# A two-layer diffusion backbone: SSD chunk exponentials issued one chunk step earlier, modulation row sums queued behind VectorE's last evacuation

## The chip, the core and the metric

One program on one core of a Trainium2 chip. A core has a matrix engine (TensorE, PE in the profile; its weight loads are PEld), VectorE (DVE), ScalarE (ACT), GpSimd (POOL) and a queue of transfers (SyncE, SP), which run beside each other and wait for one another through semaphores. Each takes its own instructions in the order in which the program queued them. The metric is the device time of one execution in microseconds (us); a kernel's time is the median of its runs.

## What is computed

The reference runs two post-norm layers over 512 latent tokens and 256 context tokens of width 1024. Layer 0 mixes tokens with gated linear attention, layer 1 with a bidirectional Mamba-2 scan (SSD); each is followed by a squared-ReLU MLP of width 4096. Every sub-layer's input is scaled and shifted, and its output gated, by vectors that come from one linear map of the conditioning. Cut to what matters here:

```python
m_l = split((silu(c) @ ada_w[i] + ada_b[i]), 6)      # latent stream
m_c = split((silu(c_ctx) @ ada_w[i] + ada_b[i]), 6)  # context stream
h = layer_norm(alpha * h + m[2] * mixer(h * (1 + m[1]) + m[0]))
h = layer_norm(alpha * h + m[5] * square(relu((h * (1 + m[4]) + m[3]) @ w1)) @ w2)
# SSD, per chunk and head; j sums over the chunk's tokens
decay = exp(where(mask, cum_i - cum_j, -inf))
y = (C_i . B_j) * decay * (x_j dt_j)  +  C_i . exp(cum_i) . state
```

There are six modulation vectors per layer (m[0] to m[5]), and two streams.

## The kernel before

All matrices are kept transposed, 128 features on the partitions and 768 tokens (512 latent, then 256 context) along the free axis. Each large product is made of three float32r products of a high and a low part: the weight is split into `wh` and `wl` (`split_to`, L211: the copy on ACT, the subtraction on VectorE), the activation into `xh` and `xl`, or `rh` and `rl` in the MLP. `prod` (L253) runs the three terms over the 8 tiles of the contraction. Weights are loaded through four `raw` buffers by SyncE, and `wh` and `wl` have three buffers each. Products land in four PSUM banks, two for a block of 768 columns.

**How work is interleaved.** The program is traced once, in Python. `worked(n)` (L188) is called after every matmul of the large products and counts their columns; each 768 columns are one unit. After a number of units that the running generator asked for, the next step of the `side` queue is traced (a LayerNorm, or the inner part of an SSD group). Every `pace[0]` units one step of the `background` queue is traced. A scheduler then gives each engine's instructions out in the order in which they become ready in its own model of the machine, earlier traced ones first among those that are ready. So an instruction that depends on little can be queued long before the place at which it was traced. `tc.issue_after(ins)` takes that freedom: what a block traces on the engine of `ins` is queued behind `ins`. It is an order of issue, not a wait for the end of `ins`.

**The MLP** (`ffn`, L382). W1 blocks go through `f1` (L387): `prod`, then `f1_out` (L392): relu from PSUM on ACT (L403), its square on POOL into `rq`, one buffer (L404), the rounded square `rh` on ACT (L405), the remainder `rl` on VectorE (L406). Batches of 8, 8, 8, 5 and 3 blocks of W1 (`bi` 0 to 4; the sizes of layer 0) are each followed by the matching part of W2 (`accum_proj`, L443), whose products are evacuated by `gated_add` (L438) with the gate of the modulation, on VectorE. In the first batch two blocks are held in PSUM, while the LayerNorm before finishes. The gate, vector (layer, 5), is asked for by `mod` (L205) at the end of the first batch; `mod` traces background steps until it is there.

**Row sums.** The modulation vectors after the first two are not made by TensorE. `ada_rows` (L143) is a background generator: for each of the eight 128-row parts of a vector it loads 128 rows of the transposed map (512 KB, three `rawa` buffers, one load ahead) and takes one multiply with row sum on VectorE per stream (L166), with the row of silu(c) broadcast in `srow`. During layer 0's mixer three vectors of layer 0 are made. At the start of layer 0's MLP the list [(0, 5), (1, 0) to (1, 5)] is queued: 56 steps, of two sums each for the first three vectors and of one for the last four, 80 sums in all. The pace is 21, then 15 after the two held blocks, then 22 from the end of the first batch on.

**The SSD layer** (`ssd_layer`, L771) has eight groups of four heads. `group(g)` (L920) projects and convolves B, C and two tiles of x (`conv`, L889: PSUM is copied out on ACT, L896, and the taps L905 and the gate L908 run on VectorE), then two gate tiles, and puts `inner(g)` (L938) on the side queue, so that it is traced between the projections of the next group. `evac[0]` always holds ACT's last evacuation. `inner` goes through four chunks of 128 latent tokens:

- `chunk_rows(c)` (L947) loads two rows of cumulated decay, broadcast over the partitions, into `L` tiles (ten buffers, two per chunk), and POOL masks them (L952). Chunks 0 and 1 are fetched at the start, chunk c + 2 in step c.
- `inter(i)` (L1020) multiplies with the running states and adds up `T`.
- `decays(c, L)` (L1032) takes the exponentials, 8 of 128x128 on ACT (L1039), with the other token's term as bias.
- `masks(c, L)` (L1041) adds the two directions on POOL (L1042) and multiplies by C.B on VectorE (L1043).
- `outputs(c, M)` (L1046) runs TensorE over the mask (L1050) and adds to `T` (L1053).

In the loop of L1058, step c traces the outputs of chunk c - 1, then the exponentials of chunk c behind `evac[0]`, then its masks. 14 units lie between steps (13 in the last group), and 4 before each `inter` (5).

Of the kernel before, what the change touches and what calls it, by code (L numbers as in the profile page):

```python
# [2 lines left out]

# [6 lines left out]
F32 = mybir.dt.float32  # L10
# [3 lines left out]
ALU = mybir.AluOpType  # L14
# [22 lines left out]
NLC = NL // P  # L37
# [23 lines left out]
def tile_backbone(ctx, tc, xT, cc, cr, vecs, rows, ada_w0, ada_wr, lnf, ffn_w1, ffn_w2,  # L61
                  gla_w_in, gla_w_v, gla_w_a, gla_a2, gla_w_out, ssd_w_in, ssd_w_dt, ssd_w_out, out):
    nc = tc.nc
# [28 lines left out]
    def part_of(ps, t0, n):  # L92
        return ps[t0 // NL][:, t0 % NL:t0 % NL + n]
# [17 lines left out]
    nc.gpsimd.memset(sT, 0.0)  # L111
    nc.scalar.activation(sT[:, :, 0:2], cin, AF.Silu)
    mods = {}

    def ada_block(src, dst, c0, rawf):
        j, b = dst.shape[1:3]
# [26 lines left out]
    def ada_rows(items, alloc, junk):  # L143
        srow = [alloc(s) for s in range(2)]
        for s in range(2):
            nc.sync.dma_start(srow[s], cr[s:s + 1, :].to_broadcast([P, D]))
            nc.scalar.activation(srow[s], srow[s], AF.Silu)
        def load(layer, m, b):
            raw = wpool.tile([P, D], F32, tag="rawa", name=nm("rawa"), bufs=3)
            nc.sync.dma_start(raw, ada_wr[48 * layer + 8 * m - 16 + b])  # L150
            return raw

        todo = [(layer, m, b) for layer, m in items for b in range(8)]
        raws = [load(*todo.pop(0))]
        yield
        for layer, m in items:
            streams = range(1 if layer and m > 1 else 2)
            t = ct([P, 8, 2], f"row{layer}{m}")
            nc.gpsimd.memset(t, 0.0)
            for b in range(8):  # L160
                if todo:
                    raws.append(load(*todo.pop(0)))
                raw = raws.pop(0)
                for s in streams:
                    o = raw if s == streams[-1] else junk()
                    nc.vector.scalar_tensor_tensor(o, raw, 1.0, srow[s], ALU.mult, ALU.mult, accum_out=t[:, b, s:s + 1])  # L166
                yield
            c0 = V_ADA + 48 * layer + 8 * m
            nc.vector.tensor_tensor(t, t, vec[:, c0:c0 + 8].unsqueeze(2).to_broadcast([P, 8, 2]), ALU.add)
            mods[layer, m] = t  # L170
# [28 lines left out]
    wait, pace = [0], [9]  # L199
# [182 lines left out]
    def ffn(layer, xs, acc, segs, pool, npre, presegs, restsegs, passes, after):  # L382
        W1, W2 = ffn_w1[layer], ffn_w2[layer]
        rs = {}
        NN = span(segs)[1]

        def f1(m, sg, hold=None):  # L387
            w, ps = hold or (weights(W1, m), mm_ps(sg))
            prod(ps, w, xs, sg, KT)
            f1_out(m, ps)  # L390

        def f1_out(m, ps):  # L392
            if m not in rs:
                rs[m] = (pool.tile([P, NN], F32R, tag="rs", name=nm("rh"), bufs=20),
                         pool.tile([P, NN], F32R, tag="rs", name=nm("rl"), bufs=20))
            rh, rl = rs[m]
            for piece in passes if m == DFF // P - 1 else (segs,):
                a, b = span(piece)
                eng = nc.gpsimd if piece is segs else nc.vector
                r = pool.tile([P, NN], F32, tag="rr", name=nm("rr"), bufs=2)  # L400
                q = pool.tile([P, NN], F32, tag="rq", name=nm("rq"), bufs=1)
                for (t0, n, _) in piece:
                    nc.scalar.activation(r[:, t0:t0 + n], part_of(ps, t0, n), AF.Relu)  # L403
                eng.tensor_mul(q[:, a:b], r[:, a:b], r[:, a:b])  # L404
                nc.scalar.activation(rh[:, a:b], r[:, a:b], AF.Square)  # L405
                nc.vector.tensor_sub(rl[:, a:b], q[:, a:b], rh[:, a:b].bitcast(F32))  # L406

        nlast = NN // 256
        h0 = 0
        for bi, nb in enumerate((8, 8, 8, 8 - nlast, nlast)):  # L410
            ms = range(h0, h0 + nb)
            if bi == 0:
                drain(1)
                held = []
                for m in ms[:npre]:
                    held.append((weights(W1, m), mm_ps(segs)))
                    prod(held[-1][1], held[-1][0], xs, presegs, KT)
                drain()
                for m in ms[:npre]:
                    f1(m, restsegs, held[m])  # L420
                pace[0] = 15
                ms = ms[npre:]
            if bi == 4:
                ws = pair_weights(W2, h0, nb,
                                  lambda j: [pool.tile([P, NN], F32R, tag="rs", name=nm("ws"), bufs=20) for _ in range(2)])
            for m in ms:
                f1(m, segs)
            ys = [rs[m] for m in range(h0, h0 + nb)]
            if bi == 0:
                gate = mod(layer, 5)  # L430
                pace[0] = 22
            if bi < 4:
                accum_proj(W2, h0, nb, ys, gate, acc, segs)
            else:
                accum_last(ws, ys, gate, acc, passes, after, early=None if layer == 0 else 5)
            h0 += nb

    def gated_add(acc, m, ps, gate, segs, src=None):  # L438
        for (t0, n, s) in segs:
            nc.vector.scalar_tensor_tensor(acc[m][:, t0:t0 + n], part_of(ps, t0, n), gate[:, m, s:s + 1],  # L440
                                           (src or acc)[m][:, t0:t0 + n], ALU.mult, ALU.add)

    def accum_proj(W, k0, kt, xs, gate, acc, segs, ms=range(KT)):  # L443
        for m in ms:
# [326 lines left out]
    def ssd_layer(xs, accd, acc0):  # L771
# [21 lines left out]
        with phase("st0") as tp:  # L793
# [14 lines left out]
            src = wload(ssd_w_dt)  # L808
            split_to(w[:, :, 0:64], w[:, :, 64:], src)
            ps = mm_ps()  # L810
# [24 lines left out]
            for c0, c1 in ((0, 4), (4, 6)):  # L835
# [3 lines left out]
                vc, n = v[:, c0:c1], c1 - c0  # L839
# [71 lines left out]
        evac = [None]  # L911
# [26 lines left out]
        def inner(g, fB, fC, fx, zs):  # L938
# [8 lines left out]
            def chunk_rows(c):  # L947
                L = [sp.tile([P, 4, P], F32, tag="L", name=nm("L"), bufs=LB) for _ in range(2)]
                for z in range(2):
                    nc.sync.dma_start(L[z].rearrange("p h i -> p (h i)"),  # L950
                                      crowc[z, c, g:g + 1].rearrange("g h i -> g (h i)").to_broadcast([P, 4 * P]))
# [7 lines left out]
            Rs, Ms = {c: chunk_rows(c) for c in range(2)}, {}  # L959
# [60 lines left out]
            def inter(i):  # L1020
                nc.scalar.activation(Es[i], Es[i], AF.Exp)
                for z in range(2):
                    E = Es[i][:, z]
                    ip = sm_ps([P, NL])
                    for c in range(NLC):
                        cs = slice(c * P, (c + 1) * P)
                        nc.tensor.matmul(ip[:, cs], ST[c][:, z, i * P:(i + 1) * P], fC[:, cs], start=True, stop=True)
                    nc.vector.tensor_mul(E if z else T[:, i], ip, E)
                nc.gpsimd.tensor_add(T[:, i], T[:, i], E)
                nc.vector.scalar_tensor_tensor(T[:, i], fx[i][:, 0:NL], dcol[:, 2 * g + i:2 * g + i + 1], T[:, i], ALU.mult, ALU.add)  # L1030

            def decays(c, L):  # L1032
                for z, t in enumerate(L):
                    if z >= ZB:
                        nc.scalar.activation(t, t, AF.Exp)
                        continue
                    for h in range(4):
                        r = 32 * z + 4 * g + h
                        nc.scalar.activation(t[:, h, :], t[:, h, :], AF.Exp, bias=lcol[:, c, r:r + 1])  # L1039

            def masks(c, L):  # L1041
                nc.gpsimd.tensor_add(L[0], L[0], L[1])  # L1042
                nc.vector.tensor_mul(L[0], L[0], cbs[:, c:c + 1, :].to_broadcast([P, 4, P]))  # L1043
                return L[0]

            def outputs(c, M):  # L1046
# [5 lines left out]
                t = T[:, :, c * P:(c + 1) * P]  # L1052
                nc.vector.tensor_add(t, t, yp)  # L1053

            for i in range(2):
                yield SSDI[g == SG - 1]
                inter(i)
            for c in range(NLC + 1):  # L1058
                yield SSDY[g == SG - 1]
                if c > 0:  # L1060
                    outputs(c - 1, Ms.pop(c - 1))
                if c < NLC:
                    L = Rs.pop(c)
                    with tc.issue_after(evac[0].ins):
                        decays(c, L)
                    Ms[c] = masks(c, L)
                if c + 2 < NLC:
                    Rs[c + 2] = chunk_rows(c + 2)
            yield 3
# [22 lines left out]
        gate = mod(1, 2)  # L1092
        acc = [apool.tile([P, NT], F32, tag="acc", name=nm("acc")) for _ in range(KT)]
# [78 lines left out]
    with phase("start") as st:  # L1172
# [15 lines left out]
        m = ct([P, 2, 8, 2], "ada01")  # L1188
        blocks = ((0,), (1,), (2, 3), (4, 5), (6, 7))
        for bi in range(6):  # L1190
            if bi < 5:
                ks = blocks[bi]
                kv = slice(ks[0], ks[0] + len(ks))
                src = ada_w0[0, 2 * bi:2 * bi + 2] if bi < 2 else ada_w0[bi - 1]
# [30 lines left out]
    acc, es, tail = gla_layer(xs, first)  # L1225
# [24 lines left out]
    acc, es, tail = ssd_layer(nxt["xs"], accd, acc0)  # L1250
# [86 lines left out]
```

## Time and profile before

| | |
|---|---|
| median of 3 runs | 1948.65 us (1946.78 to 1952.36) |
| the profiled execution's own time | 1946.43 us |
| its span, first to last instruction | 1944.7 us |
| mean granted TensorE clock | 0.993 |
| exponentials, L1039 ACT | 256, 78.5 us busy, mean 392 ns |
| add of directions, L1042 POOL | 32, 49.5 us, mean 1548 ns |
| row sums, L166 VectorE | 80 and 48 (into the other output), 101.0 and 61.8 us |
| HBM traffic over the span | 209.07 MB read, 8.13 MB written |

The profile is one execution, recorded by the chip. Its views: the page (busy time per engine, then the costliest groups of instructions by source line); waits (who stood idle for whom: total, times, longest); busy time by stretches of the span, with the clock that TensorE was granted; and instructions in order of time. In the last a row has its start in us from the start of the span, its length, engine, line, operation and tiles, and in brackets the engine's idle time before it and what ended that.

### The profile page before, as it was taken

The numbers are of one execution on the slowest core, as the hardware profiler recorded it, in microseconds if no ns is written. First come the engines' busy times: TensorE is split into PE (matmuls) and PEld (weight loads), VectorE is DVE, ScalarE is ACT, GpSimd is POOL, SyncE is SP. The second block draws the span as 40 slices with busy tenths as digits, with TensorE's granted clock in tenths as the row PEclk, the third lists the DMA queues.
The fourth block names the chain that finished last, engine by engine and source line by source line (L and its number), as shares of the span: only waits on it lengthen the run. The fifth ranks groups of instructions, "written<-read, shape, count | busy, mean of one in ns | idle before, by whom it ended". The sixth has DMA issues, their size and how long they took to land.

```text
span 1944.7 us, 28804 instructions
## 1 busy us (share of the span) xinstructions
PE 1870.5 (96%) x11365; PEld 1596.9 (82%) x11365; DVE 1265.5 (65%) x1932; ACT 797.8 (41%) x1387; POOL 411.6 (21%) x363
## 2 busy tenths in 40 slices
PE   7989999999899999999999999999999999999997
PEld 5978888788788888888897777787777888888886
DVE  4899777978976222224477888888896673333345
ACT  4445456455212213122274555446555452323231
POOL 2033241202102102000002433233432311102012
PEclk9999999999999999999999999999999999999999
DMA  9624203123686222113225433334433523333321
GB/s 353 191 73 133 77 26 99 44 84 115 223 263 201 65 66 64 58 48 98 65 77 126 138 111 104 118 115 130 131 112 127 166 74 97 98 98 98 95 84 60
DMA packets 78999, 219.07 MB, mean 113 GB/s; under 512 B 11088, under 2 KB 15824, under 8 KB 78864
## 3 DMA queue, kind: packets, MB, share of 16 engines
q1 hardware_dynamic: 78864, 217.24, 35.6%
q8 instruction: 89, 1.46, 0.3%
q14 instruction: 46, 0.38, 0.1%
HBM read 209.07 MB, written 8.13 MB: 112 GB/s over the span
## 4 chain that ended last, share of the span: by engine, by line
PE 59%; DVE 22%; issue 6%; ACT 5%; DMA 4%; POOL 3%; SPq 1%; DVEq 0%; ACTq 0%; POOLq 0%
PE mm L259 51%; DVE cv L905 3%; DVE wl L213 2%; DMA rawa<-in_ada_wr_dram 2%; DVE junk L166 2%; DVE rawa L166 2%; DVE cf L908 2%; DVE A L614 1%; PE sm L697 1%; POOL W L633 1%; PE mm L541 1%; DMA raw<-in_ada_w_dram 1%; DVE acc L440 1%; ACT wh L212 1%; DVE E L625 1%
## 5 line engine op out<-in xcount | busy, mean ns | idle before, releaser
L259 PE MATMUL mm<-xh,wh 128*128 128x512 f32 (+1 forms) x1800 | 548.0, 358 | 3.7 <-ACT xh L1085 1.9
L259 PE MATMUL mm<-xl,wh 128*128 128x512 f32 (+1 forms) x1800 | 544.2, 355 | 1.1 <-DVE xl L1086 1.1
L259 PE MATMUL mm<-xh,wl 128*128 128x512 f32 (+1 forms) x1800 | 542.4, 354 | 2.1 <-DVE wl L213 2.1
L212 ACT CAST wh<-raw 128x1024 fp32r<-128x1024 f32 (+3 forms) x225 | 226.5, 1008 | 675.0 <-PE mm L259 660.0
L213 DVE TENSOR_TENSOR wl<-raw,wh 128x1024 fp32r<-128x1024 f32 (+3 forms) x225 | 272.1, 1211 | 198.2 <-ACT wh L212 194.3
L259 PEld LDWEIGHTS mm<-xh,wh 128*128 128x128 f32 x1800 | 299.9, 189 | 56.2 <-issue 4.9
L259 PEld LDWEIGHTS mm<-xl,wh 128*128 128x128 f32 x1800 | 299.5, 189 | 50.5 <-issue 3.4
L259 PEld LDWEIGHTS mm<-xh,wl 128*128 128x128 f32 x1800 | 299.0, 189 | 51.0 <-DVE wl L213 3.0
L404 POOL TENSOR_TENSOR rq<-rr 128x768 f32<-128x768 f32 (+1 forms) x62 | 106.8, 1722 | 734.1 <-ACT rr L403 675.7
L440 DVE SCALAR_TENSOR_TENSOR acc<-mm,row,acc 128x256 f32<-128x256 f32 (+1 forms) x182 | 100.7, 580 | 205.3 <-PE mm L259 204.9
L259 PE MATMUL mm<-rl,wh 128*128 128x512 f32 x704 | 212.4, 355 | 5.4 <-DVE rl L406 5.4
L259 PE MATMUL mm<-rh,wh 128*128 128x512 f32 x704 | 212.1, 355 | 0.0
L259 PE MATMUL mm<-rh,wl 128*128 128x512 f32 x704 | 212.0, 355 | 0.0
L905 DVE SCALAR_TENSOR_TENSOR cv<-pre,cvec,cv 128x770 f32<-128x770 f32 (+1 forms) x128 | 146.1, 1141 | 14.5 <-ACT cv L903 12.8
L259 PEld LDWEIGHTS mm<-rl,wh 128*128 128x128 f32 x704 | 116.0, 189 | 25.3 <-DVE rl L406 5.7
L259 PEld LDWEIGHTS mm<-rh,wl 128*128 128x128 f32 x704 | 115.8, 188 | 19.7
L259 PEld LDWEIGHTS mm<-rh,wh 128*128 128x128 f32 x704 | 115.9, 188 | 19.5
L166 DVE SCALAR_TENSOR_TENSOR rawa<-rawa,srow 128x1024 f32<-128x1024 f32 x80 | 101.0, 1278 | 17.9 <-DMA rawa<-in_ada_wr_dram 17.4
L406 DVE TENSOR_TENSOR rl<-rq,rh 128x768 fp32r<-128x768 f32 (+2 forms) x67 | 53.2, 794 | 65.3 <-POOL rq L404 65.0
L952 POOL TENSOR_SCALAR_AFFINE_SELECT L<-L 128x512 f32<-128x512 f32 x64 | 58.7, 921 | 97.6 <-DMA L<-crowc 70.7
L1039 ACT ACTIVATE L<-L,lcol 128x128 f32<-128x128 f32 x256 | 78.5, 392 | 0.0
L907 ACT ACTIVATE cf<-cv 128x512 f32<-128x512 f32 (+1 forms) x56 | 27.6, 533 | 92.5 <-DVE cv L905 92.5
(295 smaller groups left out, 2544.3 us busy)
## 6 DMA issues: line engine op xcount, KB each, us to landing
raw<-in_ffn_w_dram SPq DMA_DIRECT2D x112, 512.0 KB, 3.8
rawa<-in_ada_wr_dram SPq DMA_DIRECT2D x80, 512.0 KB, 4.4
raw<-in_ssd_w_in_dram SPq DMA_DIRECT2D x48, 512.0 KB, 3.8
L<-crowc SPq DMA_DIRECT2D x64, 256.0 KB, 3.7
raw<-in_ada_w_dram SPq DMA_DIRECT2D x16, 512.0 KB, 9.2
raw<-in_gla_w_in_dram SPq DMA_DIRECT2D x16, 512.0 KB, 4.5
ec<-crow SPq DMA_DIRECT2D x64, 128.0 KB, 2.9
acc<-in_xT_dram SPq DMA_DIRECT2D x14, 384.0 KB, 6.9
```

The lines of the kernel that those rows point to most:

```text
L166: nc.vector.scalar_tensor_tensor(o, raw, 1.0, srow[s], ALU.mult, ALU.mult, accum_out=t[:, b, s:s + 1])
L212: nc.scalar.copy(h, src)
L213: nc.vector.tensor_sub(l, src, h.bitcast(F32))
L259: nc.tensor.matmul(part_of(ps, t0, n), a[:, k, :], b[:, t0:t0 + n], start=(k == 0 and i == 0), stop=(k == kt - 1 and i == 2))
L404: eng.tensor_mul(q[:, a:b], r[:, a:b], r[:, a:b])
L406: nc.vector.tensor_sub(rl[:, a:b], q[:, a:b], rh[:, a:b].bitcast(F32))
L440: nc.vector.scalar_tensor_tensor(acc[m][:, t0:t0 + n], part_of(ps, t0, n), gate[:, m, s:s + 1], (src or acc)[m][:, t0:t0 + n], ALU.mult, A ...
L905: nc.vector.scalar_tensor_tensor(c[:, 0:n], pre[:, t:t + n], cw(t), c[:, 0:n], ALU.mult, ALU.add)
L907: nc.scalar.activation(f[:, t0:t1], c[:, t0 + d:t1 + d], AF.Tanh)
L908: nc.vector.scalar_tensor_tensor(f[:, t0:t1], f[:, t0:t1], 1.0, c[:, t0 + d:t1 + d], ALU.add, ALU.mult)
L952: nc.gpsimd.affine_select(out=L[z], in_=L[z], compare_op=ALU.is_ge, fill=NEG, base=0, pattern=[[0, 4], [1 - 2 * z, P]], channel_multiplier ...
L1039: nc.scalar.activation(t[:, h, :], t[:, h, :], AF.Exp, bias=lcol[:, c, r:r + 1])
```

## The change

Three edits:

- `evacv[0]` remembers VectorE's last evacuation: the `rl` subtraction in `f1_out`, or the last `gated_add`. The row sums of `ada_rows` are traced under `issue_after` of it (where there is one already; there is none while layer 0's mixer runs its row sums).
- The pace of the background after the two held blocks goes from 15 to 19, and stays 22 later.
- In `inner`, the exponentials of chunk 0 are traced right after `inter(0)`, and those of chunk c + 1 in step c, after the masks of chunk c. Each is behind the `evac[0]` of that moment, as before. Masks, outputs and row fetches stay in their steps.

```diff
+    evacv = [None]
+
+    def behind():
+        return tc.issue_after(evacv[0].ins) if evacv[0] else nullcontext()
...
                 for s in streams:
                     o = raw if s == streams[-1] else junk()
-                    nc.vector.scalar_tensor_tensor(o, raw, 1.0, srow[s], ALU.mult, ALU.mult, accum_out=t[:, b, s:s + 1])
+                    with behind():
+                        nc.vector.scalar_tensor_tensor(o, raw, 1.0, srow[s], ALU.mult, ALU.mult, accum_out=t[:, b, s:s + 1])
...
-                nc.vector.tensor_sub(rl[:, a:b], q[:, a:b], rh[:, a:b].bitcast(F32))
+                evacv[0] = nc.vector.tensor_sub(rl[:, a:b], q[:, a:b], rh[:, a:b].bitcast(F32))
...
-                pace[0] = 15
+                pace[0] = 19
...
-            nc.vector.scalar_tensor_tensor(acc[m][:, t0:t0 + n], part_of(ps, t0, n), gate[:, m, s:s + 1],
-                                           (src or acc)[m][:, t0:t0 + n], ALU.mult, ALU.add)
+            evacv[0] = nc.vector.scalar_tensor_tensor(acc[m][:, t0:t0 + n], part_of(ps, t0, n), gate[:, m, s:s + 1],
+                                                      (src or acc)[m][:, t0:t0 + n], ALU.mult, ALU.add)
...
+            def ahead(c):
+                with tc.issue_after(evac[0].ins):
+                    decays(c, Rs[c])
+
             for i in range(2):
                 yield SSDI[g == SG - 1]
                 inter(i)
+                if i == 0:
+                    ahead(0)
             for c in range(NLC + 1):
                 yield SSDY[g == SG - 1]
                 if c > 0:
                     outputs(c - 1, Ms.pop(c - 1))
                 if c < NLC:
-                    L = Rs.pop(c)
-                    with tc.issue_after(evac[0].ins):
-                        decays(c, L)
-                    Ms[c] = masks(c, L)
+                    Ms[c] = masks(c, Rs.pop(c))
+                if c + 1 < NLC:
+                    ahead(c + 1)
                 if c + 2 < NLC:
                     Rs[c + 2] = chunk_rows(c + 2)
```

More of the change, by code (lines that the diff above doesn't have):

```diff
@@ L1 @@
 import math
-from contextlib import ExitStack
+from contextlib import ExitStack, nullcontext
 import concourse.bass as bass
```

## The prediction, made before the change was built or timed

> **What bounds the kernel now.** I read the page first, then TensorE's own waits, then busy time by stretches, then the order of time around TensorE's two kinds of long wait. The page's first lines:
>
> ```profile
> span 1944.7 us, 28804 instructions
> PE 1870.5 (96%) x11365; PEld 1596.9 (82%) x11365; DVE 1265.5 (65%) x1932; ACT 797.8 (41%) x1387; POOL 411.6 (21%) x363
> ```
>
> TensorE works 96% of the span, so an edit can win only what TensorE loses: 1944.7 - 1870.5 = 74 us of standing, and stretches at a reduced clock. The view of waits, TensorE alone (total, times, longest), and the same for 431 to 990 us, the first MLP (last two rows):
>
> ```profile
> PE sm L1050 <- DVE L L1043: 9.1, 6, 1.5
> ...
> PE mm L259 <- DVE rl L406: 5.4, 1, 5.4
> ...
> PE sm L1050 <- issue: 2.4, 1, 2.4
> ...
> PE sm L917 <- ACT Bn L918: 1.8, 6, 0.4
> ...
> PE mm L259 <- DVE acc L440: 1.0, 1, 1.0
> PE mm L259 <- ACT wh L212: 0.8, 1, 0.8
> ```
>
> Both halves of the diff aim at rows here. L1050 multiplies by an SSD mask and waits for it 6 + 1 times. The rl wait is one of 5.4 us in the first MLP. The stretches:
>
> ```profile
> 500.00:550.00 50.00, 44.65 (x245) 38.65 (x244) 47.77 (x79) 6.87 (x8) 2.95 (x2) 0.93 0.73 239
> 550.00:600.00 50.00, 48.13 (x275) 41.41 (x274) 36.39 (x61) 9.08 (x12) 2.17 (x1) 1.00 0.80 260
> 650.00:700.00 50.00, 50.00 (x290) 43.73 (x289) 14.50 (x19) 6.69 (x7) 1.31 (x1) 1.00 0.21 64
> 1100.00:1150.00 50.00, 48.20 (x275) 39.32 (x273) 44.72 (x68) 25.64 (x55) 13.53 (x12) 1.00 0.40 119
> ```
>
> Columns after the length: PE, PEld, DVE, ACT, POOL busy, granted clock, DMA share, GB/s. An undisturbed stretch of this MLP passes 290 matmuls in 50 us. A 512 and a 256 column matmul make one unit of 768 columns, so a unit of the kernel's own count is 50/145 = 0.345 us.
>
> **Row sums in the first MLP.** VectorE, then ACT, POOL and PE, at the end of the first eight W1 blocks, and the group of the sums with its first and last start:
>
> ```profile
> 505.11 0.87 ACT L403 ACTIVATE rr<-mm 128x512 f32<-128x512 f32 x2
> 508.46 2.32 POOL L404 TENSOR_TENSOR rq<-rr 128x768 f32<-128x768 f32 x1 [7.83 <-DVE rl L406]
> 507.37 0.95 DVE L406 TENSOR_TENSOR rl<-rq,rh 128x768 fp32r<-128x768 f32 x1
> 508.24 1.21 DVE L166 SCALAR_TENSOR_TENSOR rawa<-rawa,srow 128x1024 f32<-128x1024 f32 x1
> ...
> 514.09 1.22 DVE L166 SCALAR_TENSOR_TENSOR rawa<-rawa,srow 128x1024 f32<-128x1024 f32 x1
> 515.23 1.21 DVE L213 TENSOR_TENSOR wl<-raw,wh 128x1024 fp32r<-128x1024 f32 x1
> 516.45 0.95 DVE L406 TENSOR_TENSOR rl<-rq,rh 128x768 fp32r<-128x768 f32 x1
> 517.46 0.79 PE L259 MATMUL mm<-rl,wh 128*128 128x512 f32 x1 [5.36 <-DVE rl L406]
> L166 DVE SCALAR_TENSOR_TENSOR rawa<-rawa,srow x80: 1211/1220/2495, 54.3 to 612.5; 128x1024 f32<-128x1024 f32 x80
> rawa<-in_ada_wr_dram SPq DMA_DIRECT2D x80, 512.0 KB, 4.4
> ```
>
> ACT has the last block's relu at 506.0, but POOL squares it only at 508.46, since its one rq buffer is held until rl of the block before (508.3). Then row sums of 1.2 us each stand in VectorE's queue ahead of the rl that TensorE wants. They need nothing but their load, so the scheduler gives them out as soon as VectorE is free in its plan, and all are done by 612.5 + 1.2.
>
> With the edge each sum is queued no earlier than the last rl or acc traced before it. By the kernel's count (clock at 696 units when this MLP starts) two advances fall in the held blocks; the 144 units of the six other blocks give 7 at pace 19 (10 at 15), and `mod(0,5)` forces one more: the gate is complete just as bi 0 ends. After that one step per 22 units, 7.6 us; the last of the 47 steps comes 47 x 7.6 = 357 us after bi 0, at about 860 us.
>
> In a W1 block of 24 units (8.3 us) VectorE then has wl 1.21 + rl 0.95 + 1.26 steps of two sums (3.1) = 5.3 us. With rl no longer behind sums, rq goes at 506.0, ends at 508.3, and rl is there at 509.3; TensorE wants it at 517.46 - 5.36 = 512.1. What is now queued behind a waiting acc or rl is the sums, then the next wl; wl is three buffers ahead of TensorE, so 2.4 us of sums in front of it cost nothing; were that lead gone, a step would cost those 2.4 us. Each step moves its 512 KB load too: SyncE takes it when one of the three rawa buffers is free, and weight loads stand behind it in that queue. Spread over 7.6 us instead of bunched they interfere less (DMA share 0.73 and 0.80 against 0.21). I price this at nothing; at worst it brings back the 0.8 us wait for wh.
>
> The gain by count of matmuls: (290 - 245) + (290 - 275) = 60, times 50/290 = **10.3 us**. By parts: 5.4 + 1.0 + 0.8 of waits, plus the clock:
>
> ```profile
> 517.46:522.00 4.54, 4.54 (x14) 3.86 (x15) 4.54 (x9) 1.05 (x1) 0.00 (x0) 0.50 0.65 217
> 1046.00:1054.00 8.00, 5.10 (x25) 4.14 (x24) 6.74 (x8) 4.41 (x8) 4.15 (x4) 0.81 0.53 205
> 1135.00:1142.00 7.00, 7.00 (x41) 5.88 (x39) 6.65 (x9) 5.94 (x17) 2.96 (x2) 1.00 0.50 142
> 1456.00:1464.00 8.00, 6.14 (x29) 4.85 (x28) 7.50 (x11) 6.28 (x13) 5.58 (x2) 0.79 0.87 278
> 1579.00:1588.00 9.00, 6.81 (x38) 5.94 (x37) 5.54 (x17) 7.42 (x15) 1.08 (x2) 0.81 0.01 2
> ```
>
> 4.54 us at 0.50 lose 2.3 us: 9.5 us in all by parts. I take 10.3 as the end above and in the sum, since those are matmuls that did not run; 7 is the end below, if one late rl of 2.4 us stays at a later change from W1 to W2. Three more places, which the change does not touch, run at 0.79 to 0.81: 8 x 0.19 + 8 x 0.21 + 9 x 0.19 = 4.9 us lost there. All after 512 us now comes 10 to 20 us earlier, and whether such short waits (TensorE stood under 3 us in each) lower the clock may change: 4.9 us either way, in the range alone.
>
> "TensorE: Matmul & The Clock Gate" of the Trainium skill (section "Why this matters for your kernels") says to allow "No PE-idle gaps >~3µs between matmul bursts": by it only the 5.4 us wait could have cost clock, and the 4.9 us would not be in play. The rows at 1046, 1456 and 1579 say otherwise, so the range goes by the rows.
>
> **Exponentials one step ahead.** One SSD group in order of time: ACT, POOL, VectorE, TensorE.
>
> ```profile
> 1125.77 1.04 ACT L903 ACTIVATE cv<-pre,cvec 128x770 f32<-128x770 f32 x1
> 1135.35 0.94 ACT L907 ACTIVATE cf<-cv 128x512 f32<-128x512 f32 x2 [8.55 <-DVE cv L905]
> 1136.20 0.57 ACT L896 COPY pre<-mm 128x512 f32<-128x512 f32 x1
> 1136.67 1.28 ACT L1039 ACTIVATE L<-L,lcol 128x128 f32<-128x128 f32 x4
> 1138.65 0.82 ACT L903 ACTIVATE cv<-pre,cvec 128x512 f32<-128x512 f32 x1 [0.70 <-DVE cf L908]
> 1139.37 3.61 ACT L1039 ACTIVATE L<-L,lcol 128x128 f32<-128x128 f32 x12
> 1140.72 1.47 POOL L1042 TENSOR_TENSOR L<-L,L 128x512 f32<-128x512 f32 x1 [2.44 <-ACT L L1039]
> 1142.66 0.68 DVE L1043 TENSOR_TENSOR L<-L,cbs 128x512 f32<-128x512 f32 x1
> 1143.60 0.44 PE L1050 MATMUL sm<-L,xnat 128*64 128x128 f32 x4 [1.52 <-DVE L L1043]
> 1142.21 0.33 SPq L950 DMA_DIRECT2D L<-crowc  x1
> L<-crowc SPq DMA_DIRECT2D x64, 256.0 KB, 3.7
> DVE L L1043 <- POOL L L1042: 13.0, 9, 1.8
> POOL L L952 <- DMA L<-crowc: 70.7, 38, 13.5
> ```
>
> Chunk 0's eight exponentials stand behind the evacuation of 1136.20; add, multiply and matmul follow, and TensorE stands 1.52 us. After the change they are traced 4 + 14 = 18 units (6.2 us) earlier, behind the evacuation before, whose conv activation is at 1125.77, with 8.55 us of idle ACT after it. There they take 8 x 3.61/12 = 2.4 us, the add 1.5, the multiply 0.7: ready at 1126.8 + 4.6 = 1131.4, ten us before TensorE wants it. Chunk 1 takes chunk 0's old place, ready at 1143.3, wanted 14 units after 1142.08, at 1146.9. Chunks 2 and 3 likewise gain 4.8 us.
>
> What is late next? TensorE comes 1.5 us earlier to the transposes of L917, which already wait 6 times, 0.3 us each, for ACT. VectorE feeds them; it is busy 44.7 of 50 us, and its waits for POOL's add (13.0 in 9) go, so it keeps up by as much or more. I allow the 1.8 us there to double. On ACT the conv activation and the weight casts queue behind exponentials that might wait for a row tile: SyncE fetches L at 1142.21, the moment POOL's add frees a tile (1140.72 + 1.47 = 1142.19), so tiles are loaded as far ahead as ten buffers allow, and I price that at nothing. POOL's add moves ahead of the adds to T, at 1129 to 1131, when POOL stands. The seven waits are those of seven groups; the eighth shows none, and nothing is priced there.
>
> Gain: 9.1 + 2.4 = 11.5, less 1.8 = **9.7 us**. Bounds: nothing, if L917 takes the waits over; 13.3, if both rows go.
>
> **Sum.** The profiled execution took 1946.43 us, 2.2 below the median. 10.3 + 9.7 = 20.0: 1926.4 for it, and 1948.65 - 20.0 = **1928.6** as a median. About 0.3%, 5.8 us, is what a measurement here tells from no change.
>
> **Rivals.**
> - *SSD keeps its pace* (0.10). VectorE becomes what ends the wait: cf is late at L917 by what L1050 saved. For it: 44.72 of 50 us busy. Against: the waits of VectorE that go. 1948.65 - 10.3 = 1938.4.
> - *The MLP keeps its wait* (0.07): rl is late from LayerNorm's work on VectorE before, or the forced step's sums come ahead of rl. Against: six sums in a row stand right before it. 1948.65 - 9.7 = 1939.0.
> - *The edges bind nothing* (0.07): the order of issue comes out as before, or the clock stretches take the gain back. 1948.
> - *ACT waits for row tiles* (0.06), slower. Rows for chunks 2 and 3 would be fetched only at their traced place, one step (4.8 us) ahead of the exponentials now: load 3.7 and POOL's selection behind its own mean wait of 70.7/38 = 1.9 us make it at least 0.8 us late, 2.6 with a second such wait, and casts and evacuations stand behind it on ACT. Two chunks, seven groups: 14 waits. It decides from 20.0/14 = 1.4 us each; at 2.6 it costs 36.4: 1928.6 + 36.4 = 1965. For it: POOL's waits for L. Against: the fetch at 1142.21.
>
> **Numbers.** Both pay: 0.70, by itself 1920 to 1936 (bounds of clock, L917 and the later rl). The first two rivals reach to 1939, so 1921 to 1939 leaves out the last two (0.13) and the edges. Faster 0.70 + 0.10 + 0.07 = 0.87; same 0.07; slower 0.06.
>
> **What would show it.** Right: no rl wait near 512, granted clock 1.00 from 500 to 550, 290 matmuls in each 50 us from 500 to 600, the last L166 near 860 rather than 612; no L1050 row among TensorE's waits; exponentials on ACT inside the 8.55 us hole. Wrong: sums still before 612; L1050's wait under another name (L917, L1027) at the same total; ACT waiting on POOL's selections ahead of L1039; new waits for wl or wh after 600.

## The result, and the profile after

| | changed kernel | kernel before, run beside it |
|---|---|---|
| median | 1938.55 us (1936.01 to 1940.55, 6 runs) | 1954.36 us (1946.78 to 1956.99, 6 runs) |
| ratio | 0.9926 (95% interval 0.9905 to 0.9948) | |
| profiled execution: time, span | 1938.47, 1936.8 us | 1946.43, 1944.7 us |

The changed kernel is faster, by 0.5 to 1.0%. The sum said 1928.6, so 10 us of the forecast gain are missing; from profile to profile it is 7.9 us instead of 20.0. (The sum started from 1948.65, the median of the first three executions of before. Against the median of all six, 1954.36, the gain is 15.8 us; the ratio is 0.9926 where 1928.6 / 1948.65 = 0.9897 was forecast. Where the difference between these counts comes from is told below.) Both halves of the change did at their places what was forecast, and the question is where the rest went. The page, first lines:

```profile
span 1936.8 us, 28836 instructions
PE 1877.8 (97%) x11365; PEld 1602.2 (83%) x11365; DVE 1265.8 (65%) x1932; ACT 795.8 (41%) x1387; POOL 392.4 (20%) x363
```

The span is 7.9 us shorter, but TensorE is *busier* by 7.3 us, 1877.8 against 1870.5, with the same 11365 matmuls. Of the 15 us that it no longer stands (74 us before, 59 now), about half went into matmuls that take longer. That is the first hint. TensorE's waits (total, times, longest):

```profile
PE sm L923 <- DVE cf L914: 4.2, 2, 3.0
PE mm L265 <- DVE xl L1097: 3.8, 2, 2.6
...
PE sm L923 <- ACT Bn L924: 2.5, 1, 2.5
...
PE mm L265 <- ACT xh L1096: 2.2, 1, 2.2
...
PE sm L1056 <- PE mm L265: 0.5, 2, 0.2
...
PE sm L1056 <- DVE L L1049: 0.4, 1, 0.4
...
PE sm L1056 <- ACT L L1045: 0.3, 1, 0.3
```

The wait for rl is gone. The mask matmul (L1056 here, L1050 before) waits 1.2 us in all, not 11.5. New are longer waits for xl and one long wait for Bn, to which we come back. The row sums, and one SSD group on ACT:

```profile
L172 DVE SCALAR_TENSOR_TENSOR rawa<-rawa,srow x80: 1212/1218/2362, 54.4 to 866.6; 128x1024 f32<-128x1024 f32 x80
```

```profile
1125.39 0.38 ACT L904 COPY pre<-mm 128x256 f32<-128x256 f32 x1
1125.65 0.41 ACT L1045 ACTIVATE L<-L,lcol 128x128 f32<-128x128 f32 x1
1125.96 1.03 ACT L909 ACTIVATE cv<-pre,cvec 128x770 f32<-128x770 f32 x1
1126.88 2.15 ACT L1045 ACTIVATE L<-L,lcol 128x128 f32<-128x128 f32 x7
1137.42 0.94 ACT L913 ACTIVATE cf<-cv 128x512 f32<-128x512 f32 x2 [8.40 <-DVE cv L911]
```

The last sum starts at 866.6 (forecast: about 860), and the eight exponentials of chunk 0 (the rows L1045) lie ahead of ACT's long idle time, behind the evacuation before. So far all is as forecast. Then the stretches, columns as before the change:

```profile
500.00:550.00 50.00, 50.00 (x285) 43.41 (x284) 29.89 (x47) 8.04 (x10) 2.80 (x2) 1.00 0.44 137
550.00:600.00 50.00, 50.00 (x285) 43.36 (x284) 28.29 (x43) 9.28 (x12) 3.48 (x2) 1.00 0.41 132
...
650.00:700.00 50.00, 50.00 (x285) 43.32 (x284) 21.75 (x33) 6.30 (x6) 0.00 (x0) 1.00 0.43 139
```

No standing and full clock from 500 to 600, as forecast, but 285 matmuls per 50 us where 290 were counted on, and 285 also from 650 to 700, where the kernel before passed 290 and the edit should matter little. In order of time, TensorE in the kernel before and then in the changed one, two matmuls to a row:

```profile
700.87 0.51 PE L259 MATMUL mm<-rh,wh 128*128 128x512 f32 x2
701.22 0.51 PE L259 MATMUL mm<-rl,wh 128*128 128x512 f32 x2
701.56 0.51 PE L259 MATMUL mm<-rh,wl 128*128 128x512 f32 x2
701.91 0.51 PE L259 MATMUL mm<-rh,wh 128*128 128x512 f32 x2
```

```profile
701.10 0.53 PE L265 MATMUL mm<-rh,wh 128*128 128x512 f32 x2
701.46 0.51 PE L265 MATMUL mm<-rl,wh 128*128 128x512 f32 x2
701.81 0.51 PE L265 MATMUL mm<-rh,wl 128*128 128x512 f32 x2
702.16 0.53 PE L265 MATMUL mm<-rh,wh 128*128 128x512 f32 x2
```

From rh,wh to the next rh,wh (six matmuls, one tile of the contraction) it is 1.04 us before and 1.06 after, with no idle time in either. From start to start a 512 column matmul takes 231 to 233 ns before, and 241, 236 and 232 ns in turn after. I call the first spacing close, the second wide. By stages, between marks that both traces have (first relu of an MLP, first matmul of the SSD's time steps, first matmul with the triangle):

| us | before | after | |
|---|---|---|---|
| layer 0's mixer | 442.1 | 443.7 | +1.6 |
| layer 0's MLP | 548.2 | 546.5 | -1.7: standing 8.5 to 1.1, half clock 2.3 to 0, the rest 537.5 to 545.4 |
| SSD, with its head | 603.2 | 595.4 | -7.8: standing 24.5 to 18.7, half clock 5.1 to 3.5 |
| layer 1's MLP | 351.2 | 351.2 | 0 |

So layer 0's MLP won 9.7 us and lost 7.9 to the wider spacing.

### The profile page after: what moved, and what is told of

Same layout as the page of the kernel before. It is cut to its first block, busy times and chain, and to the rows that moved or that the text cites. A ratio compares the mean times of both kernels' runs of the same rounds, so it can differ in the third digit from the quotient of the medians.

```text
span 1936.8 us, 28836 instructions
## 1 busy us (share of the span) xinstructions
PE 1877.8 (97%) x11365; PEld 1602.2 (83%) x11365; DVE 1265.8 (65%) x1932; ACT 795.8 (41%) x1387; POOL 392.4 (20%) x363
## 4 chain that ended last, share of the span: by engine, by line
PE 60%; DVE 17%; issue 9%; ACT 6%; POOL 4%; DMA 4%; SPq 1%; DVEq 0%; ACTq 0%; POOLq 0%
PE mm L265 53%; DVE cv L911 4%; DMA L<-crowc 2%; DVE cf L914 2%; DVE wl L219 1%; DVE A L620 1%; PE sm L703 1%; POOL L L1048 1%; POOL W L639 1%; PE mm L547 1%; DVE E L631 1%; DMA raw<-in_ada_w_dram 1%; POOL ssum L1089 1%; DVE lnst L330 1%; ACT xn L340 1%
## 5 line engine op out<-in xcount | busy, mean ns | idle before, releaser
L410 POOL TENSOR_TENSOR rq<-rr 128x768 f32<-128x768 f32 (+1 forms) x62 | 102.4, 1652 | 735.5 <-ACT rr L409 732.7
L1045 ACT ACTIVATE L<-L,lcol 128x128 f32<-128x128 f32 x256 | 80.1, 393 | 0.0
L1048 POOL TENSOR_TENSOR L<-L,L 128x512 f32<-128x512 f32 x32 | 49.0, 1530 | 151.1 <-ACT L L1045 151.1
L958 POOL TENSOR_SCALAR_AFFINE_SELECT L<-L 128x512 f32<-128x512 f32 x64 | 53.6, 838 | 119.5 <-DMA L<-crowc 111.1
```

The costliest lines, as they stand in the source:

```text
L958: nc.gpsimd.affine_select(out=L[z], in_=L[z], compare_op=ALU.is_ge, fill=NEG, base=0, pattern=[[0, 4], [1 - 2 * z, P]], channel_multiplier ...
```

## The experiments

Each kernel ran beside the kernel before on one chip; the first four, the next four and the last three shared a chip and its runs of before (medians 1953.08 of 26 runs, 1954.09 of 20, 1949.18 of 18). These are three different chips, so times of kernels from different sets are better compared by their ratios to before.

**Whose is the spacing?** Both kernels once more, and each half alone. The theory that led: the spacing differs from one execution to the next and is no effect of the edit. Its rival: the new order sets it.

Before, unchanged:

> The kernel before, unchanged, profiled once more beside the other three. Lead theory (the closer or wider spacing of matmuls in layer 0's MLP is no effect of the edit; it differs from one execution or chip to the next): the count of matmuls per 50 us between 600 and 900 us may come out at 285 or at 290, and its time goes with it (near 1948 us with 290, near 1956 with 285). Rival (the changed order sets the spacing): 290 again, 512 column matmuls started every 232 ns.

1953.31 us (1945.43 to 1955.98, 12 runs), ratio 1.0 (0.9984 to 1.0016). The profiled execution took 1955.98, and its windows show both spacings in one execution:

```profile
524.00:574.00 50.00, 50.00 (x291) 44.10 (x289) 41.91 (x73) 6.33 (x6) 0.00 (x0) 1.00 0.80 263
592.00:642.00 50.00, 50.00 (x285) 43.40 (x284) 27.41 (x38) 16.00 (x24) 12.05 (x6) 1.00 0.47 150
```

It is close up to 578.2 us, where a weight load of the next block comes late and a matmul with it, by 0.1 us, and wide from there to the end of the MLP. In the first profile of this same kernel, 1946.43 us, the spacing turns wide at the same place too, behind the 0.8 us for wh, and turns close again behind the wait for acc at 588; from 592 to 642 it passes 291. The rival ("290 again") fell with that: the order of work is one and the same in both. The same wait for acc comes in the longer execution too, 0.5 us at 587.6, but leaves the spacing wide.

Changed, unchanged:

> The changed kernel, unchanged, profiled once more. Lead theory: the same count per 50 us between 600 and 900 us as the kernel before shows in this call, whichever it is, and a ratio to it near 0.991 (18 us). Rival: 285 again, 512 column matmuls every 236 to 241 ns, while the kernel before keeps 290, and a ratio near 0.996 (8 us) against a kernel before with 290.

1940.73 us (1935.82 to 1944.05, 7 runs), ratio 0.994 (0.9918 to 0.9962), between the two that were expected; 285 again, all through the MLP.

Edges and pace alone (the first two edits of the diff, the third left out; against the kernel before, cut):

```diff
-                    nc.vector.scalar_tensor_tensor(o, raw, 1.0, srow[s], ALU.mult, ALU.mult, accum_out=t[:, b, s:s + 1])
+                    with behind():
+                        nc.vector.scalar_tensor_tensor(o, raw, 1.0, srow[s], ALU.mult, ALU.mult, accum_out=t[:, b, s:s + 1])
...
-                pace[0] = 15
+                pace[0] = 19
```

> The edges of the row sums and pace 19 alone; the SSD loop as before. Both theories: no rl wait near 512, no stretch at half clock there, last row sum near 866 us, the L1050 waits of 11.5 us kept. Lead theory: the spacing is that of the kernel before in this call and the kernel is 10 us faster than it. Rival: 285 matmuls per 50 us from 600 to 900 us where the kernel before has 290, and 2 to 3 us faster only.

1946.51 us (1944.45 to 1948.96, 12 runs), ratio 0.9973 (0.996 to 0.9985). Spacing 285; MLP 546.5 us, of which TensorE stood 1.1.

The exponentials ahead alone (the third edit, the first two left out; against the kernel before, cut):

```diff
             for i in range(2):
...
+                if i == 0:
+                    ahead(0)
...
-                    with tc.issue_after(evac[0].ins):
-                        decays(c, L)
...
+                if c + 1 < NLC:
+                    ahead(c + 1)
```

> The exponentials one step ahead alone; row sums at pace 15 without edges. Both theories: the rl wait of 5.4 us and the half clock behind it stay, the L1050 waits fall from 11.5 to about 1 us, and the kernel is 6 to 8 us faster than the one before (11.5 less what the traces of the changed kernel gave back: 2.3 us more waits for cf and Bn, about 3 us at the end of the SSD stage). Rival: 290 matmuls per 50 us from 600 to 900 us in every execution, since the order there is that of before; lead theory: 285 or 290, as the kernel before in this call.

1942.57 us (1938.29 to 1947.75, 8 runs), ratio 0.9953 (0.9933 to 0.9973). The rl wait of 5.35 us is there, the L1050 waits are 1.0 us, and the spacing is 290. By its ratio the gain is about 9 us, more than the 6 to 8 expected. The SSD stage without its head took 569.7 us, against 574.6 and 579.0 in the two profiles of before.

What follows: the halves add up within their intervals (0.27% and 0.47%, against 0.74% and 0.60% for both), but neither theory holds as it was put. Without the edges both spacings occur; with them all three profiles so far are wide. The traces show why that may be: in the profiles without edges a matmul comes late at four places (463 us for wl, 512 for rl, 578 for wh, 588 for acc), and the spacing changes only there. With the edges TensorE stands nowhere between 446 and 957 us, and the wide spacing with which it leaves the LayerNorm's transposes stays. So a new theory, which the next runs test: **the spacing is settled where the regular stream of matmuls is broken, and kept until the next break.**

**Break the stream of the changed kernel.** First by a wait, with the changed kernel's rl of one block computed six times:

```diff
-                evacv[0] = nc.vector.tensor_sub(rl[:, a:b], q[:, a:b], rh[:, a:b].bitcast(F32))
+                for _ in range(6 if layer == 0 and m == 7 else 1):
+                    evacv[0] = nc.vector.tensor_sub(rl[:, a:b], q[:, a:b], rh[:, a:b].bitcast(F32))
```

> The changed kernel, with the rl of the eighth W1 block of layer 0 computed six times over (same values): VectorE ends it near 515.3 instead of 510.5, so TensorE must stand about 1.4 us at the eighth k of the first W2 block, the place where the kernel before stood 5.36. New lead theory (the spacing pattern is settled where TensorE's stream restarts after standing, and kept until it stands again): the stretch after 516 runs at 230 to 232 ns per 512 columns (290 per 50 us) in some or all executions, as behind that wait in all three profiles that have it, and the median falls by up to 8 - 1.5 = 6 us, with runs spread over 1931 to 1941. Rival (the order of VectorE's work, spread or bunched row sums, sets the spacing): 285 per 50 us as in the changed kernel, and 1.5 us slower than it, 1941.

1933.06 us (1929.91 to 1940.88, 6 runs), ratio 0.9895 (0.9875 to 0.9915). With added work and an added wait most executions are shorter than those of the changed kernel (1935.8 to 1944.1 in its two runs, on other chips): four took 1929.9 to 1934.0, two 1939.7 and 1940.9. The profiled one is one of these two; it stood 0.85 us for rl (1.4 expected), and is wide on both sides. So a break may also lead from wide to wide.

Then by a matmul that waits for nothing:

```diff
             prod(ps, w, xs, sg, KT)
+            if layer == 0 and m == 7:
+                d = sm_ps([P, P])
+                nc.tensor.transpose(d, ident, ident)
             f1_out(m, ps)
```

> The changed kernel with one more 128x128 transpose on TensorE, of a constant that is always there, behind the eighth W1 block of layer 0 (its result is not used): the stream is shifted by 0.1 us but does not stand. If it takes standing to settle the pattern: 236 before and after it, 285 per 50 us, the time of the changed kernel within 0.3%. If any break of the regular stream will do: 230 to 232 behind it in some executions.

1933.64 us (1930.1 to 1940.19, 6 runs), ratio 0.9897 (0.988 to 0.9914). Five runs took 1930.1 to 1934.5, which speaks for any break; but the profiled one, 1940.19, is again wide on both sides, so no trace shows it yet. The same kernel was run again for a profile of a shorter execution.

> The changed kernel with the one transpose more, once more, for a profile of an execution that is one of its shorter ones (five of six runs took 1930 to 1934.5 us, the profiled one 1940.2 with 236 ns before and behind the transpose). If the spacing is what parts them: an execution near 1932 shows 285 per 50 us ahead of the transpose at 506 us and 288 to 291 behind it, with net time of the MLP down by 7 to 8 us; an execution near 1940 shows 285 on both sides. If it is something else: 285 on both sides in an execution near 1932.

1933.63 us (1931.03 to 1939.26, 5 runs), ratio 0.9926 (0.9899 to 0.9953; before's median was lower on this chip, where 10 of its 18 executions were below 1950). The profiled execution took 1932.29. TensorE around the added transpose (L398):

```profile
501.89 0.52 PE L265 MATMUL mm<-xh,wh 128*128 128x512 f32 x2
...
502.95 0.52 PE L265 MATMUL mm<-xh,wh 128*128 128x512 f32 x2
...
504.02 0.27 PE L398 MATMUL sm<-ident 128*128 128x128 f32 x1
...
504.48 0.51 PE L265 MATMUL mm<-rl,wh 128*128 128x512 f32 x2
...
505.52 0.51 PE L265 MATMUL mm<-rl,wh 128*128 128x512 f32 x2
```

1.06 us for six matmuls ahead of it, 1.04 behind it, in one execution. The windows of this execution, and then of the other one of the same kernel:

```profile
463.00:503.00 40.00, 40.00 (x229) 34.68 (x228) 28.33 (x39) 11.79 (x19) 8.86 (x5) 1.00 0.48 151
510.00:550.00 40.00, 40.00 (x233) 34.99 (x232) 25.43 (x40) 5.26 (x5) 0.00 (x0) 1.00 0.41 132
650.00:700.00 50.00, 50.00 (x291) 43.71 (x290) 20.83 (x32) 6.31 (x6) 0.00 (x0) 1.00 0.44 138
```

```profile
463.00:503.00 40.00, 40.00 (x229) 34.69 (x228) 28.53 (x38) 13.14 (x20) 9.02 (x6) 1.00 0.50 158
510.00:550.00 40.00, 40.00 (x228) 34.76 (x227) 24.62 (x39) 5.26 (x5) 0.00 (x0) 1.00 0.42 138
650.00:700.00 50.00, 50.00 (x285) 43.46 (x284) 21.48 (x33) 5.81 (x6) 0.00 (x0) 1.00 0.41 137
```

The same instructions, full clock and no standing in both: 538.1 us for the MLP in one, 546.6 in the other. This 8.5 us is the spacing alone, and since the kernel is the same in both, neither the order of its work nor the added transpose by itself decides which spacing an execution gets.

The transpose in the kernel with edges and pace only:

> Edges and pace, the one transpose more behind the eighth W1 block, and the SSD loop as before. Spacing theory: most runs 6 to 8 us below the same kernel without the transpose (1946.5), so 1938 to 1941, a few at 1946; 290 per 50 us behind the transpose where the profiled run is one of the short ones. If the transpose helped by the SSD loop's order or by chance of the session: 1946 throughout.

1937.01 us (1935.44 to 1949.35, 12 runs), ratio 0.9948 (0.993 to 0.9966). Eight runs lie at 1935.4 to 1938.0, the other four at 1940.7 to 1949.4; the same kernel without the transpose lay at 1944.4 to 1949.0 throughout (on another chip, with a ratio of 0.9973). The profile (1935.44 us) shows 290 from 650 to 700, and an MLP of 538.1 us.

**Edges or pace?** Each of the two alone, without the third edit; the cuts are against the kernel with edges and pace. First the edges:

```diff
-                pace[0] = 19
+                pace[0] = 15
```

> The edges on the row sums alone, pace 15 as before, SSD loop as before. The sums can no longer stand ahead of rl, so no rl wait near 512; more steps fall in the first blocks (10 instead of 7), the last sum stays near 866, since the pace after them is the same. Time as with edges and pace (0.997 of the kernel before), spacing 236 for want of a wait.

1947.09 us (1944.34 to 1950.52, 9 runs), ratio 0.9967 (0.9953 to 0.9981). No wait for rl, wl or acc in the MLP, 285 per 50 us. The last sum came at 845.5, not 866: that part of the expectation forgot that three steps earlier in the first batch are three fewer later (3 x 7.6 = 23 us).

Then the pace:

```diff
-                    with behind():
-                        nc.vector.scalar_tensor_tensor(o, raw, 1.0, srow[s], ALU.mult, ALU.mult, accum_out=t[:, b, s:s + 1])
+                    nc.vector.scalar_tensor_tensor(o, raw, 1.0, srow[s], ALU.mult, ALU.mult, accum_out=t[:, b, s:s + 1])
```

> Pace 19 alone, no edges, SSD loop as before. Without edges the scheduler gives the sums out as soon as VectorE is free in its plan: the rl wait near 512 stays at 4 to 6 us, half clock behind it, last sum near 612, time that of the kernel before within 0.3%, its spacing 232 or 236 by execution.

1949.11 us (1945.32 to 1958.32, 12 runs), ratio 0.9986 (0.9969 to 1.0002). Its waits from 440 to 980 us, and its sums:

```profile
PE mm L259 <- DVE rl L406: 4.9, 1, 4.9
PE mm L259 <- DVE acc L440: 1.1, 1, 1.1
PE mm L259 <- ACT wh L212: 0.8, 1, 0.8
```

```profile
L166 DVE SCALAR_TENSOR_TENSOR rawa<-rawa,srow x80: 1208/1222/2492, 54.6 to 612.2; 128x1024 f32<-128x1024 f32 x80
```

The pace by itself changes nearly nothing: where a step is traced does not say when the scheduler gives its work out. The edges do the MLP's part.

**The SSD stage's give-back.** TensorE's xh and xl waits at the stage's end were 1.9 + 1.1 us before and are 2.2 + 3.8 now. The rows of the kernel before, for the waits shown above after the change:

```profile
PE sm L917 <- DVE cf L908: 3.5, 2, 2.9
...
PE mm L259 <- ACT xh L1085: 1.9, 1, 1.9
...
PE mm L259 <- DVE xl L1086: 1.1, 2, 0.6
```

It is xl that grew: over all profiles its wait is 1.1 to 2.0 us in the six with the SSD loop of before, and 3.7 to 4.1 in the six with all groups ahead (xh: 1.9 to 3.3, and 2.2 to 2.3). SyncE and VectorE there, in the changed kernel:

```profile
1441.58 0.42 SPq L1108 DMA_DIRECT2D yl<-yrow  x1
1446.35 0.92 SPq L1085 DMA_DIRECT2D yrow<-y  x2
1447.32 5.31 SPq L1108 DMA_DIRECT2D yl<-yrow  x4
```

```profile
1441.09 4.17 DVE L911 SCALAR_TENSOR_TENSOR cv<-pre,cvec,cv 128x770 f32<-128x770 f32 x4
...
1445.63 1.29 DVE L1083 SCALAR_TENSOR_TENSOR y<-T,zs 128x512 f32<-128x512 f32 x2
...
1451.07 0.74 DVE L1097 SCALAR_TENSOR_TENSOR xl<-yl,vec,xh 128x512 fp32r<-128x512 f32 x1
```

The second yl load stands in SyncE's queue behind group 6's two writes of y, these wait for VectorE's y, and y comes behind 4.2 us of convolution; so xl is there at 1451.8. To see whether group 6's exponentials, given out ahead, bring that about, the kernel with the transpose got them only in groups 1 to 5. Group 0 is left out too, because its gain came to nothing: TensorE at the change of group behind it, before and after:

```profile
1114.63 0.87 PE L917 MATMUL sm<-ident,cf 128*128 128x128 f32 x6 [0.28 <-ACT Bn L918]
```

```profile
1114.66 0.87 PE L923 MATMUL sm<-ident,cf 128*128 128x128 f32 x6 [2.49 <-ACT Bn L924]
```

Its wait for the mask went from 2.39 to 0.26 us, but VectorE and ACT come to this place no earlier than before (VectorE's second y at 1111.33 and 1111.36), so TensorE waits here instead. The edit:

```diff
-                if i == 0:
+                if i == 0 and 0 < g < SG - 2:
                     ahead(0)
...
                 if c < NLC:
+                    if not 0 < g < SG - 2:
+                        ahead(c)
                     Ms[c] = masks(c, Rs.pop(c))
-                if c + 1 < NLC:
+                if c + 1 < NLC and 0 < g < SG - 2:
                     ahead(c + 1)
```

> The changed kernel with the one transpose more, and the exponentials ahead only in groups 1 to 5; groups 0, 6 and 7 as before. If the longer waits at the group change after group 0 (Bn, 2.0 to 2.6 us instead of 0.3 to 0.8) and at the end of the SSD stage (xh and xl, 4.8 to 5.2 us instead of 2.4 to 3.8, and 3.4 us more at half clock) come from the exponentials given out ahead in groups 0 and 6: they go back to the values of before, the L1050 waits of these two groups (2.4 and 1.5 us) come back, and the sum is 0 to 2 us in favour. If they come from VectorE's place in the whole loop: they stay, and the kernel is 4 us slower than with the transpose alone.

1929.76 us (1927.26 to 1937.87, 6 runs), ratio 0.9904 (0.9881 to 0.9926), 3.9 us below the kernel with the transpose alone, beside which it ran (1933.63); 0 to 2 were expected. Its waits from 1000 to 1600 us:

```profile
PE sm L926 <- DVE cf L917: 4.2, 2, 3.8
...
PE sm L1059 <- issue: 2.4, 1, 2.4
PE mm L265 <- ACT xh L1101: 2.2, 2, 2.0
PE mm L265 <- DVE xl L1102: 2.1, 3, 0.9
PE sm L1059 <- DVE L L1052: 1.5, 1, 1.5
```

The Bn wait of over 2 us is gone, xl takes 2.1 instead of 4.1 us, there is no half clock at the stage's end, and groups 0 and 6 wait for their masks again (2.4 and 1.5). So the longer waits for Bn and xl do come from the groups at both ends. What leaving these groups out is worth is less sure. The stage took 566.1 us, against 571.1 with all groups ahead, but 4.8 of these 5.0 us are half clock (3.2 against 8.0), which differs as much between other profiles; TensorE stands 16.8 us in it instead of 18.5. The medians also differ by the share of short executions (five of six here, three of five there), and the two intervals of the ratio overlap. Of the versions run this has the lowest median, but not the lowest ratio to before.

All profiles, for the account below (us; the SSD stage without its head, and TensorE's standing in the MLP):

| profile of | its time | MLP of layer 0 | standing in it | matmuls, 650 to 700 | SSD stage |
|---|---|---|---|---|---|
| before | 1946.43 | 548.2 | 8.5 | 290 | 574.6 |
| before again | 1955.98 | 553.5 | 7.1 | 285 | 579.0 |
| pace only | 1946.78 | 548.2 | 8.0 | 290 | 575.1 |
| exponentials only | 1938.29 | 546.4 | 7.2 | 290 | 569.7 |
| changed | 1938.47 | 546.5 | 1.1 | 285 | 566.9 |
| changed again | 1935.82 | 546.5 | 1.1 | 285 | 567.0 |
| edges and pace | 1948.96 | 546.5 | 1.1 | 285 | 577.2 |
| edges only | 1947.46 | 546.5 | 1.1 | 285 | 576.8 |
| changed, rl six times | 1939.65 | 547.6 | 1.9 | 285 | 568.6 |
| changed, transpose | 1940.19 | 546.6 | 1.1 | 285 | 569.2 |
| changed, transpose, again | 1932.29 | 538.1 | 1.1 | 291 | 571.1 |
| edges and pace, transpose | 1935.44 | 538.1 | 1.1 | 290 | 574.9 |
| groups 1 to 5, transpose | 1927.26 | 538.1 | 1.1 | 291 | 566.1 |

## Why the prediction was right in direction and short in size

**The MLP's term, 10.3 us: the step that failed.** What the edges should do, they did: no rl wait, full clock, the last sum at 866.6. The step that failed is the unit the gain was counted in, "an undisturbed stretch of this MLP passes 290 matmuls in 50 us". An undisturbed stretch passes 290 or 285, and taking every wait away took away what might lead from 285 to 290. The sum looked at the 100 us in which the waits lay, but the wider spacing runs through the whole stage: 9.7 us of standing and half clock were won there, and 7.9 lost. The term measured 548.2 - 546.5 = 1.7 us against the profile that the sum was made against. Against an execution of before that turned wide (553.5) it is 7.0. With the close spacing on both sides for most of the stage (before, and the kernels with the transpose) it is 548.2 - 538.1 = 10.1 us.

**The SSD's term, 9.7 us.** The waits for masks fell by 11.5 - 1.2 = 10.3. At L923 (L917 before) cf and Bn together went from 3.5 + 1.8 to 4.2 + 2.5, so 1.4 of the 1.8 us that were allowed were used. That the allowance fits is luck: it was made for six short waits for Bn that double, and what came is one wait of 2.5 behind group 0, with which L1050's wait there went on under another name. What the sum put at nothing is the end of the stage: xh and xl wait 6.0 us instead of 3.0. Standing fell by 5.8 us and half clock by 1.6, 7.4 of the 7.7 from profile to profile; over all profiles the stage is shorter by 576.3 - 568.8 = 7.5 (six with the loop of before, six with all groups ahead). "Nothing is priced there" was said of the eighth group; the price was at the group before it.

**The sum.** Forecast 20.0, measured 7.9 from profile to profile: 8.6 short in the MLP, 2.0 in the SSD, and 1.6 in the mixer of layer 0, which no edit reaches before its end. Two stretches at half clock there, at 165.0 and 219.7 us, are in this profile and not in the second one of the same kernel (mixer 440.9 us). The measured median, 1938.55, lies on the figures of two rivals, 1938.4 and 1939.0, and neither of them happened as a whole: the SSD did not keep its pace but for group 0, and the MLP did not keep its wait. That the median lies in the stated range of 1921 to 1939 is therefore luck. A total can be met by a mechanism that is not there; only the waits tell.

**The clock.** The term of 4.9 us either way was in the range alone, and it was right to have one: over the 13 profiles half clock costs the SSD stage 1.7 to 8.0 us, and two profiles of one kernel differ by up to 3.3 (4.7 and 8.0). The changed kernel at the end of the stage, where a wait of 2.2 us ends at 1448.4 and another of 2.7 us follows within the stretch:

```profile
1448.50:1455.30 6.80, 4.15 (x16) 3.28 (x16) 5.71 (x7) 2.93 (x6) 1.48 (x2) 0.50 0.63 194
```

The rule of the Trainium skill that stood in the prediction ("TensorE: Matmul & The Clock Gate", section "Why this matters for your kernels": "No PE-idle gaps >~3µs between matmul bursts") does not cover this stretch either: no single wait here reaches 3 us.

**The median.** Before's own median moved from 1948.65 to 1953 or 1954 and back to 1949. By its times, most of which lie below 1950 or above 1952, it moved with the share of executions that turn wide in the MLP; only two of them were profiled (1946.43, close for the most part, and 1955.98, wide). That is a reason to compare ratios from one chip, and profiles by stage.

**What stays open.** Why there are two spacings, and what decides which one follows a break, is not known. Behind a break both occur: by their times 8 of 11 runs of the changed kernel with the transpose were short, and three of the four profiles with the transpose are close behind it. That the wait in the repeated rl leads to the close spacing is read from its times alone, as its one profile stayed wide. That the writes of y delay yl is read from the queue; only the effect of the groups was tried. How much of the half clock in the SSD stage is the edit's is open too.

## What to carry to other kernels

Before you count a gain in matmuls per stretch, take the spacing in several stretches and several executions; a stream without waits need not run at the spacing that it has between waits. Split the difference of two traces into standing, clock and spacing by stage before you look for a cause: here the first two came out as forecast, and the third hid it. An order edge kept work out of another's way here where pacing alone did not. Work moved ahead gains only where what comes next can move too: in the groups at both ends its gain came back as other waits.

## What the runs showed of the hardware

The same float32r matmuls, with no idle time and at a granted clock of 1.00, ran in layer 0's MLP at two rates for hundreds of us: 290 or 291 per 50 us (from start to start 230 to 233 ns for 512 columns) or 285 (232 to 241 ns). Behind one 128x128 transpose between two blocks it went from 285 to 290 or 291 for the rest of the stage in three profiles of four, and stayed at 285 in the fourth; between two executions of one and the same kernel this made 8.5 us. In layer 1's MLP, which has 512 columns only, it was 227 ns in every profile.

The Trainium skill, "TensorE: Matmul & The Clock Gate" (section "Wait — 56ns, not 53.3ns?"), gives a start-to-start time for a warm clock of 215.7 ns at N = 512. The traces here show 227 to 241 ns for these float32r matmuls, and two rates.
